# Strided attention: an output partition with 16 queries of two heads, and the turned weights in a block matrix

## The chip, the cores and the metric

The kernel runs on one core of a Trainium2 chip. The metric is the device time of one execution in microseconds; of the kernel before there are three runs. One further execution was recorded by the profiler; the views below are of that one. A core has four compute engines, each with its own queue of instructions: TensorE (PE, matmuls), VectorE (DVE), ScalarE (ACT) and GpSimd (POOL). SyncE (SP) issues the transfers, which 16 DMA engines carry out.

## The reference

Each query attends to every 64th position alone, 16 keys per head:

```python
# Q, K, V: (8, 12, 1024, 64) float32; stride = 64
scale = 1.0 / np.sqrt(64)
for i in range(1024):
    k = K[:, :, 0:1024:stride]          # 16 keys of a head
    v = V[:, :, 0:1024:stride]
    scores = einsum('bhqd,bhkd->bhqk', Q[:, :, i:i+1], k) * scale
    weights = exp(scores - max(scores))
    weights = weights / (sum(weights) + 1e-10)
    result[:, :, i] = einsum('bhqk,bhkd->bhqd', weights, v)
```

Q is read and the result written in full, 24 MiB each. Of K and V only the rows in use are read, 384 KB each.

## The kernel before

The 96 heads are cut into 24 groups of four (`HG = 4`). A group's queries are 4 x 1024 rows of 64 numbers, 1 MiB; they lie in HBM one after the other, so partition p of a query tile `qn` holds 32 successive queries of one head, and each head takes 32 partitions. There are ten query tiles (`QBUFS`) and eight output tiles (`OBUFS`). Each group passes these steps; the names are those of the code:

1. `load`: SP moves the group's queries to `qn`.
2. `cast`: to bf16 in `qb`, a quarter on ACT and three quarters on POOL, in an order that puts the four heads' queries beside each other. `transpose`: VectorE turns blocks of 32 x 32 (pairs of bf16 as int32) into `qt`.
3. `scores`: PE, sixteen matmuls (eight tiles of 128 queries by the even and odd halves of the 64 dimensions) against the group's keys in `k_t`, 64 columns each (four heads x 16 keys), into one PSUM bank `sc`.
4. `lowered`: VectorE takes the maximum of each 16 and subtracts it; `raised`: ACT's exponential; `sums`: VectorE's sums and reciprocals; `weights`: POOL multiplies, giving bf16 weights `wn`, 128 x 512.
5. `across`: PE, four matmuls turn `wn` block by block against a permutation matrix `spread`, so that (head, key) lies along the partitions and queries along the columns. Two tiles of 64 (head, key) rows lie one below the other in each block, in the PSUM bank `wt_ps`.
6. `weight_rows`: ACT copies `wt_ps` to `wt` in bf16 (one instruction, L443).
7. `outputs` (L453): PE, eight matmuls. The stationary operand is one tile's 64 rows x 128 queries of `wt`, the moving operand the same 64 rows of `vm`, a matrix in which each head's 16 value rows stand in that head's columns and zeros elsewhere (64 rows x 256 columns, in two copies one below the other). The result, 128 queries x four heads x 64, goes to half a bank of `o_ps`. The first four matmuls fill two banks (key `o0`), the others the remaining two (`o1`).
8. `evict` (L466): ACT copies two banks at a time to the output tile, two instructions of 1024 columns.
9. `store`: SP writes the tile, alone in the first ten groups, mostly two groups at once after that. An output partition holds 8 queries of each of the four heads, so a store writes runs of 8 x 64 x 4 bytes = 2 KiB in HBM.

The groups overlap. In turn `i` the program writes out, in this order: `weight_rows(i)`, `transpose(i + 3)`, `cast(i + 4)`, `sums(i + 1)`, `scores(i + 2)`, `lowered(i + 2)`, `values(i + 1)`, `weights(i + 1)`, `outputs(i)`, `evict(i)`, `raised(i + 2)`, `across(i + 1)`, then the loads and stores. Every engine works through its own part of that order without overtaking. So ACT's queue in a turn is the weight copy, the cast, the two evictions, the exponential; PE's is scores, output products, turning. The class `Program` derives the semaphore waits from the tiles that each step reads and writes. PE and VectorE run the middle turns as a hardware loop of two turns (`PERIOD = 2`); the other engines' instructions are written out. The products of `outputs(i)` wait on the semaphore `evened`, which `weight_rows(i)` raises; the first eviction waits for the first four products and, from the ninth group on, for the store that last used the output tile.

Ahead of the loop stand the set-up of the constants (`identity`, `perm_v`, `spread`, `mask`, the cleared `k_t`), the keys' way into `k_t` (`key_rows`, `keys`), and `value_rows`, in which four matmuls of 384 columns (L344) copy the value rows to all partitions that need them.

Of the kernel before, what the change touches and what calls it, by code (L numbers as in the profile page):

```python
# [10 lines left out]
FP32 = mybir.dt.float32  # L11
BF16 = mybir.dt.bfloat16
# [190 lines left out]
def kernel(  # L203
# [8 lines left out]
    nc = tc.nc  # L212

    B, H, S, D = Q.shape
    NK = S // stride
    scale = 1.0 / math.sqrt(D)

    P = 128
    HG = 4
    NG = B * H // HG  # L220
    NC = NG // 2
    SD = S * D
    HK = HG * NK
    NT = 8
    PERIOD = 2
    assert B * H == NG * HG and S == 1024 and D == 64 and NK == 16 and NG % PERIOD == 0
    QBUFS = 10
    OBUFS = 8
    AHEAD = 4

    sb = ctx.enter_context(tc.tile_pool(name="sb", bufs=1))
# [6 lines left out]
    identity = sb.tile([P, P], BF16, name="identity")  # L238
    qn = [sb.tile([P, 32 * D], FP32, name=f"qn{i}") for i in range(QBUFS)]
    qb = [sb.tile([P, 32 * D], BF16, name=f"qb{i}") for i in range(2)]  # L240
    out_all = [sb.tile([P, 2, HG, NT, D], FP32, name=f"out_sb{i}") for i in range(OBUFS // 2)]
    out_sb = [out_all[i // 2][:, i % 2] for i in range(OBUFS)]
    qt = [sb.tile([P, 32 * D], BF16, name=f"qt{i}") for i in range(2)]
    low = [sb.tile([P, NT * HG, NK], FP32, name=f"low{i}") for i in range(2)]
    ex = [sb.tile([P, NT * HG, NK], FP32, name=f"ex{i}") for i in range(2)]
    wn = [sb.tile([P, NT * HG, NK], BF16, name=f"wn{i}") for i in range(2)]
    wt = [sb.tile([P, NT // 2, P], BF16, name=f"wt{i}") for i in range(2)]
    top = sb.tile([P, NT * HG], FP32, name="top")
    total = sb.tile([P, NT * HG], FP32, name="total")
    rec = [sb.tile([P, NT * HG], FP32, name=f"rec{i}") for i in range(2)]  # L250
    vm = [sb.tile([P, HG, D], BF16, name=f"vm{i}") for i in range(2)]
    k_t = sb.tile([P, NG, 2, HK], BF16, name="k_t")
    k_r = sb.tile([P, NC, D], BF16, name="k_r")
    v_bf = sb.tile([P, NC, D], BF16, name="v_bf")
    v_rep = sb.tile([P, NC, 2, D], BF16, name="v_rep")
    perm_v = sb.tile([P, 2, 2, HK], BF16, name="perm_v")
    spread = sb.tile([P, P], BF16, name="spread")
    s_sel = sb.tile([P, HG], BF16, name="s_sel")
    mask = sb.tile([P, HG, D], BF16, name="mask")
    sc_ps = [ps.tile([P, 512], FP32, name=f"sc{i}") for i in range(2)]  # L260
    wt_ps = [ps.tile([P, 512], FP32, name=f"wt_ps{i}") for i in range(2)]
    o_ps = ps.tile([P, 4, 512], FP32, name="o")

    prog = Program(nc, tc, PERIOD, (NG - 4) // PERIOD)
    op = prog.op
    stored = {}
    did = {}
# [17 lines left out]
    for g in range(1, QBUFS):  # L285
# [4 lines left out]
        out=identity, in_=identity, compare_op=ALU.not_equal, fill=1.0, base=0,  # L290
        pattern=[[-1, P]], channel_multiplier=1,
    ), reads=["identity"], writes=["identity"])
    for c in range(2):
        op("POOL", lambda c=c: nc.gpsimd.tensor_copy(
            out=perm_v[:, c],
            in_=identity[:, HK * c : HK * c + HK].unsqueeze(1).to_broadcast([P, 2, HK]),
        ), reads=["identity"], writes=[f"perm{c}"])
    op("POOL", lambda: nc.gpsimd.tensor_copy(
        out=spread.rearrange("p (q j) -> p q j", j=4),
        in_=identity.rearrange("p (j q) -> p q j", j=4),  # L300
    ), reads=["identity"], writes=["spread"])
    op("DVE", lambda: nc.vector.memset(k_t, 0.0),  # L302
       writes=[f"k_t{m}{c}{s}" for m in range(2) for c in range(2) for s in range(4)])
    op("DVE", lambda: nc.vector.tensor_reduce(
        out=s_sel, in_=identity.rearrange("p (h s k) -> p s h k", h=2, s=4),
        op=ALU.max, axis=mybir.AxisListType.XY,
# [16 lines left out]
    def keys(m, c, s):  # L323
        part = halves[m]
        hd = 2 * (s % 2) + s // 2
        src, dst, col = 32 * (2 * c + s % 2), 32 * hd, NK * hd
        e, fn = (
            ("DVE", nc.vector.tensor_copy) if m else
            ("POOL", nc.gpsimd.tensor_copy) if s >= 2 else ("ACT", nc.scalar.copy)
        )  # L330
        op(e, lambda: fn(  # L331
            k_t[dst : dst + 32, 2 * part.start + c : 2 * part.stop : 2, :, col : col + NK],
            k_r[src : src + 32, part].rearrange(
                "p n (a k f) -> p a n f k", a=2, f=2
            )[:, s // 2],
        ), reads=[f"k_r{m}"] + ["mask", "turn"] * (e == "POOL"),
           writes=[f"k_t{m}{c}{s}"] + ["turn"] * (e == "POOL"))

    def value_rows(n):
        rows = o_ps[:, 2 * n : 2 * n + 2, 0 : NC // 2 * D].rearrange("p c (n d) -> p c n d", d=D)  # L340

        def sums():
            for c in range(2):
                r = nc.tensor.matmul(  # L344
                    rows[:, c], lhsT=perm_v[:, c].rearrange("p a k -> p (a k)"),
                    rhs=v_bf[:, 6 * n : 6 * n + 6], start=True, stop=True,
                )
            return r

        i = op("PE", sums, reads=["v_bf", "perm0", "perm1"],  # L350
               writes=[f"o{n}"], gates=[did["v_bf"]], gate="scored")
        op("DVE", lambda: nc.vector.tensor_copy(  # L352
            out=v_rep[:, 6 * n : 6 * n + 6].rearrange("p n c d -> p c n d"), in_=rows
        ), reads=[f"o{n}"], writes=[f"v_rep{n}"], gates=[i])
# [5 lines left out]
            op=ALU.mult,  # L360
        ), reads=["mask", "v_rep0", "v_rep1"], writes=[f"vm{g % 2}"])

    cut = 6

    def cast(g):
        q = qn[g % QBUFS].rearrange("p (j t d) -> p t j d", j=4, t=NT)
        b = qb[g % 2].rearrange("p (t j d) -> p t j d", t=NT, j=4)
        one = op("ACT", lambda: nc.scalar.copy(b[:, cut:], q[:, cut:]),  # L368
                 reads=[f"qn{g % QBUFS}1"], writes=[f"qb{g % 2}1"], gate="copied")
        two = op("POOL", lambda: nc.gpsimd.tensor_copy(out=b[:, :cut], in_=q[:, :cut]),  # L370
                 reads=[f"qn{g % QBUFS}0"] + ["turn"] * (g < 2),
                 writes=[f"qb{g % 2}0"] + ["turn"] * (g < 2), gate="cast")
        did["cast", g] = [one, two]
# [8 lines left out]
    def scores(g, i=None):  # L382
        def products(i=None):
            k = g if i is None else i + 2
            q = qt[g % 2]
            for x in range(NT):
                t = x // 4 * 4 + x % 2 * 2 + x // 2 % 2
                for f in range(2):
                    r = nc.tensor.matmul(  # L389
                        sc_ps[g % 2][:, HK * x : HK * x + HK],  # L390
                        lhsT=q[:, 4 * D * t + f : 4 * D * (t + 1) : 2],
                        rhs=k_t[:, k, f], start=f == 0, stop=f == 1,
                    )
# [46 lines left out]
            gates=[did["weighed", g]], turn=i)  # L440

    def weight_rows(g):
        did["evened", g] = op("ACT", lambda: nc.scalar.copy(  # L443
            wt[g % 2], wt_ps[g % 2].rearrange("p (b q) -> p b q", b=NT // 2),
        ), reads=[f"wt_ps{g % 2}"], writes=[f"wt{g % 2}"], gate="evened")

    def outputs(g, i=None):
        for n in range(2):
            def products(i=None, n=n):
                for x in range(4 * n, 4 * n + 4):  # L450
                    b, side = x // 2, x % 2
                    rows = slice(HK * side, HK * side + HK)
                    r = nc.tensor.matmul(  # L453
                        o_ps[:, 2 * n + side, HG * D * (b % 2) : HG * D * (b % 2 + 1)],
                        lhsT=wt[g % 2][rows, b],
                        rhs=vm[g % 2][rows].rearrange("p h d -> p (h d)"),
                        start=True, stop=True,
                    )
                return r

            op("PE", products, reads=[f"wt{g % 2}", f"vm{g % 2}"], writes=[f"o{n}"],
               gates=[] if n else [did["evened", g]], turn=i)

    def evict(g):
        for n in range(2):
            op("ACT", lambda n=n: nc.scalar.copy(  # L466
                out_sb[g % OBUFS][:, :, 4 * n : 4 * n + 4].rearrange("p h t d -> p t h d"),
                o_ps[:, 2 * n : 2 * n + 2].rearrange("p b (t h d) -> p (b t) h d", t=2, h=HG),
            ), reads=[f"o{n}"], writes=[f"out{g % OBUFS}{n}"],
               after=[stored[g - OBUFS]] if g >= OBUFS and not n else [],  # L470
               last=n == 1 and g + 1 == NG)

    def send(g, n):
        o = out_sb[g % OBUFS]
        return _copy(
            nc,
            _ap_with(out, [[NT * D, P], [SD, HG * n], [1, NT * D]], g * HG * SD),
            _ap_with(o, [o.ap[0], [1, 1], [1, 32 * n * D]]),
        )

# [100 lines left out]
```

## Time and profile before

| | us |
|---|---|
| median of three runs | 129.01 (128.92 to 129.18) |
| the profiled execution | 128.92 |
| its span in the profile | 127.1 |

| Engine | busy us | share of the span |
|---|---|---|
| DVE | 88.9 | 70% |
| ACT | 86.6 | 68% |
| POOL | 78.5 | 62% |
| PE | 63.6 | 50% |
| DMA queue of SP | | 96.7% of 16 engines |

The span is the time from the first to the last instruction that the profile holds; the rest of an execution's time lies around it. In rows of instructions, the line of the code comes with the engine and the operation, then the tiles (output <- inputs) and their sizes as partitions x elements. `128*128` or `64*128` beside a matmul is the part of the PE array that it takes, rows first. In a row of the timeline, the first number is the start in us from the span's beginning, the second the duration; `x8` means that eight instructions stand in one row, and a bracket gives idle time ahead of it and what ended it. In a row of the waits stand the total in us, the number of times and the longest one. The ends of matmuls are modelled, their starts are recorded.

### The profile page before, as it was taken

How to read it: one execution, taken by the hardware profiler on the slowest of the kernel's cores; microseconds unless marked ns; L12 is line 12 of the kernel's file. 1: busy time of each engine (PE TensorE's matmuls, PEld its weight loads, DVE VectorE, ACT ScalarE, POOL GpSimd, SP SyncE). 2: the span in 40 equal slices, each digit the busy share in tenths (PEclk: the TensorE clock that was granted, in tenths of full speed). 3: DMA queues.
4: the chain of work that ended last, by engine and by line, in shares of the span. 5: the costliest groups of instructions: out<-in, count | busy, mean ns of one | idle time of the engine just before them, and what ended most of it. 6: DMA issues, size and time to landing. Idle time of an engine off the chain costs nothing.

```text
span 127.1 us, 2044 instructions
## 1 busy us (share of the span) xinstructions
PE 63.6 (50%) x676; PEld 41.9 (33%) x676; DVE 88.9 (70%) x134; ACT 86.6 (68%) x127; POOL 78.5 (62%) x87
## 2 busy tenths in 40 slices
PE   0003607658576766857766564564565477450000
PEld 0002405535254543624544334244244245220000
DVE  4259899998898989989898965965966895500000
ACT  4431316998989899898998568577586977775000
POOL 4264789898787888878789747748649433320000
DMA  2998999999999799999999899898999999999991
GB/s 50 411 433 371 474 433 392 495 392 428 433 392 495 322 405 454 392 438 446 392 456 456 361 487 433 356 490 363 436 407 433 428 412 420 418 418 423 399 415 41
DMA packets 6853, 51.17 MB, mean 402 GB/s; under 512 B 3776, under 2 KB 3776, under 8 KB 3776
## 3 DMA queue, kind: packets, MB, share of 16 engines
q1 hardware_dynamic: 6848, 51.12, 96.7%
q14 instruction: 4, 0.03, 0.1%
q8 instruction: 1, 0.02, 0.0%
HBM read 25.95 MB, written 25.17 MB: 402 GB/s over the span
## 4 chain that ended last, share of the span: by engine, by line
DMA 38%; ACT 21%; PE 10%; DVE 10%; POOL 5%; issue 4%; SPq 2%; ACTq 0%; DVEq 0%; POOLq 0%
DMA out_dram<-out_sb 31%; ACT out_sb L466 16%; DMA qn<-in_Q_dram 7%; PE o L453 4%; PE sc L389 3%; POOL wn L423 3%; ACT ex L411 3%; DVE total L416 3%; DVE qt L378 3%; PE wt_ps L432 2%; ACT wt L443 2%; DVE rec L419 2%; DVE v_rep L352 1%; POOL qb L370 1%; SPq L34 1%
## 5 line engine op out<-in xcount | busy, mean ns | idle before, releaser
L466 ACT COPY out_sb<-o 128x1024 f32<-128x1024 f32 x48 | 46.2, 1015 | 16.1 <-DMA out_dram<-out_sb 8.8
L423 POOL TENSOR_TENSOR wn<-ex,rec 128x512 bf16<-128x512 f32 x24 | 25.4, 1057 | 25.9 <-DVE rec L419 25.9
L370 POOL CAST qb<-qn 128x1536 bf16<-128x1536 f32 x24 | 35.2, 1468 | 3.8 <-DMA qn<-in_Q_dram 3.7
L389 PE MATMUL sc<-k_t,qt 128*128 (+1 forms) x384 | 25.8, 242 | 14.9 <-DVE qt L378 10.4
L453 PE MATMUL o<-vm,wt 64*128 64x256 bf16 x192 | 24.8, 411 | 14.8 <-ACT wt L443 14.7
L378 DVE STREAM_TRANSPOSE qt<-qb 128x1024 int32<-128x1024 int32 x24 | 29.8, 1240 | 2.9 <-POOL qb L370 1.5
L389 PEld LDWEIGHTS sc<-k_t,qt 128*128 128x128 bf16 x384 | 23.2, 131 | 18.1 <-DVE qt L378 10.4
L416 DVE TENSOR_REDUCE total<-ex 128x32 f32<-128x512 f32 x24 | 16.2, 674 | 12.8 <-ACT ex L411 12.8
L432 PE MATMUL wt_ps<-spread,wn 128*128 128x128 bf16 x96 | 14.6, 307 | 19.0 <-POOL wn L423 19.0
L368 ACT CAST qb<-qn 128x512 bf16<-128x512 f32 x24 | 15.2, 635 | 5.4 <-DMA qn<-in_Q_dram 5.4
L411 ACT ACTIVATE ex<-low 128x512 f32<-128x512 f32 x24 | 15.4, 642 | 4.3 <-DVE low L405 4.3
L432 PEld LDWEIGHTS wt_ps<-spread,wn 128*128 128x128 bf16 x96 | 8.3, 131 | 30.1 <-POOL wn L423 30.1
L453 PEld LDWEIGHTS o<-vm,wt 64*128 64x128 bf16 x192 | 10.5, 127 | 21.2 <-ACT wt L443 17.7
L405 DVE TENSOR_TENSOR low<-sc,top 128x512 f32<-128x512 f32 x24 | 16.6, 692 | 0.8
L357 POOL TENSOR_TENSOR vm<-mask,v_rep 128x256 bf16<-128x256 bf16 x24 | 16.1, 670 | 0.0
L402 DVE TENSOR_REDUCE top<-sc 128x32 f32<-128x512 f32 x24 | 15.2, 633 | 0.0
L443 ACT CAST wt<-wt_ps 128x512 bf16<-128x512 f32 x24 | 14.1, 587 | 0.0
L419 DVE RECIPROCAL rec<-total 128x32 f32<-128x32 f32 x24 | 8.5, 353 | 0.8
L302 DVE MEMSET k_t<- 128x1536 uint32 x1 | 1.3, 1338 | 1.9 <-issue 1.9
L344 PE MATMUL o<-v_bf,perm_v 128*128 128x384 bf16 x4 | 1.5, 521 | 2.3 <-POOL v_bf L501 2.3
L316 ACT CAST k_bf<-k_raw 128x256 bf16<-128x256 f32 (+1 forms) x2 | 0.9, 508 | 2.3 <-DMA k_raw<-in_K_dram 2.3
L331 POOL COPY k_t<-k_r 32x128 bf16<-32x128 bf16 x4 | 1.1, 288 | 2.1 <-DVE k_r L318 2.0
(17 smaller groups left out, 11.0 us busy)
## 6 DMA issues: line engine op xcount, KB each, us to landing
qn<-in_Q_dram SPq DMA_DIRECT2D x24, 1024.0 KB, 19.1
out_dram<-out_sb SPq DMA_DIRECT2D x12, 1024.0 KB, 19.6
out_dram<-out_sb SPq DMA_DIRECT2D x6, 2048.0 KB, 19.6
k_raw<-in_K_dram SPq DMA_DIRECT2D x1, 384.0 KB, 4.0
v_raw<-in_V_dram SPq DMA_DIRECT2D x1, 384.0 KB, 6.5
```

The lines of the kernel that those rows point to most:

```text
L357: op("POOL", lambda: nc.gpsimd.tensor_tensor(out=vm[g % 2], in0=mask, in1=v_rep[:, g // 2, g % 2].unsqueeze(1).to_broadcast([P, HG, D]), o ...
L370: two = op("POOL", lambda: nc.gpsimd.tensor_copy(out=b[:, :cut], in_=q[:, :cut]), reads=[f"qn{g % QBUFS}0"] + ["turn"] * (g < 2), writes=[ ...
L378: "DVE", lambda: nc.vector.transpose(qt[g % 2].bitcast(I32), qb[g % 2].bitcast(I32)),
L389: r = nc.tensor.matmul(sc_ps[g % 2][:, HK * x : HK * x + HK], lhsT=q[:, 4 * D * t + f : 4 * D * (t + 1) : 2], rhs=k_t[:, k, f], start=f == ...
L405: op("DVE", lambda: nc.vector.tensor_tensor(out=low[g % 2], in0=sc, in1=top.unsqueeze(2).to_broadcast([P, NT * HG, NK]), op=ALU.subtract,) ...
L411: did["raised", g] = op("ACT", lambda: nc.scalar.activation(out=ex[g % 2], in_=low[g % 2], func=AF.Exp, bias=0.0, scale=scale,), reads=[f" ...
L416: added = op("DVE", lambda: nc.vector.tensor_reduce(out=total, in_=ex[g % 2], op=ALU.add, axis=mybir.AxisListType.X,), reads=[f"ex{g % 2}" ...
L423: did["weighed", g] = op("POOL", lambda: nc.gpsimd.tensor_tensor(out=wn[g % 2], in0=ex[g % 2], in1=rec[g % 2].unsqueeze(2).to_broadcast([P ...
L432: r = nc.tensor.matmul(wt_ps[g % 2][:, P * b : P * b + P], lhsT=w[:, P * b : P * b + P], rhs=spread, start=True, stop=True,)
L443: did["evened", g] = op("ACT", lambda: nc.scalar.copy(wt[g % 2], wt_ps[g % 2].rearrange("p (b q) -> p b q", b=NT // 2),), reads=[f"wt_ps{g ...
L453: r = nc.tensor.matmul(o_ps[:, 2 * n + side, HG * D * (b % 2) : HG * D * (b % 2 + 1)], lhsT=wt[g % 2][rows, b], rhs=vm[g % 2][rows].rearra ...
L466: op("ACT", lambda n=n: nc.scalar.copy(out_sb[g % OBUFS][:, :, 4 * n : 4 * n + 4].rearrange("p h t d -> p t h d"), o_ps[:, 2 * n : 2 * n + ...
```

## The change

The pairing of queries and heads changes from the cast on. A tile of 128 queries is now taken so that an output partition ends up with 16 queries of two heads (`NU = 16`) where it had 8 of four; a store then writes runs of 16 x 64 x 4 bytes = 4 KiB. The four heads of a group are handled as two pairs, and for that:

- the casts' orders, `spread`, the columns of the keys in `k_t`, the value permutation `perm_v` (four small copies, not two) and the PSUM columns of the scores follow the new order; each pair of score products still fills 64 columns, now in two runs of 32;
- `wt` becomes a block matrix: for each of four blocks and both halves `u` of its queries, 128 rows x 128 columns, in which the rows 0 to 63 have data in the columns 0 to 63 and the rows 64 to 127 in the columns 64 to 127. The rest is zero, from one VectorE memset ahead of the loop (`wt_all`);
- `weight_rows` fills the two diagonal blocks with one ACT copy each, of 64 partitions x 512; the second one raises `evened`;
- `outputs` still has eight matmuls of 256 columns, but each uses all 128 rows;
- `evict` and `store` follow the new layout; the number and the size of the evictions, loads and stores stay.

```diff
+    NU = 16
...
-    out_all = [sb.tile([P, 2, HG, NT, D], FP32, name=f"out_sb{i}") for i in range(OBUFS // 2)]
+    out_all = [sb.tile([P, 2, 2, NU, D], FP32, name=f"out_sb{i}") for i in range(OBUFS // 2)]
...
-    wt = [sb.tile([P, NT // 2, P], BF16, name=f"wt{i}") for i in range(2)]
+    wt_all = sb.tile([P, 2, NT // 2, 2, P], BF16, name="wt_all")
+    wt = [wt_all[:, i] for i in range(2)]
...
+    id_v = identity.rearrange("p (c b a k) -> p c b a k", c=2, b=2, a=2)
     for c in range(2):
-        op("POOL", lambda c=c: nc.gpsimd.tensor_copy(
-            out=perm_v[:, c],
-            in_=identity[:, HK * c : HK * c + HK].unsqueeze(1).to_broadcast([P, 2, HK]),
-        ), reads=["identity"], writes=[f"perm{c}"])
+        for a in range(2):
+            op("POOL", lambda c=c, a=a: nc.gpsimd.tensor_copy(
+                out=perm_v[:, c, a],
+                in_=id_v[:, c, :, a].unsqueeze(1).to_broadcast([P, 2, 2, NK]),
+            ), reads=["identity"], writes=[f"perm{c}{a}"])
     op("POOL", lambda: nc.gpsimd.tensor_copy(
-        out=spread.rearrange("p (q j) -> p q j", j=4),
-        in_=identity.rearrange("p (j q) -> p q j", j=4),
+        out=spread.rearrange("p (u q h) -> p u q h", u=2, h=2),
+        in_=identity.rearrange("p (u h q) -> p u q h", u=2, h=2),
     ), reads=["identity"], writes=["spread"])
...
+    op("DVE", lambda: nc.vector.memset(wt_all, 0.0), writes=[f"wt{i}" for i in range(2)])
...
-        src, dst, col = 32 * (2 * c + s % 2), 32 * hd, NK * hd
+        src, dst, col = 32 * (2 * c + s % 2), 32 * hd, 32 * (s // 2) + NK * (s % 2)
...
-    cut = 6
+    cut = 12
...
-        q = qn[g % QBUFS].rearrange("p (j t d) -> p t j d", j=4, t=NT)
-        b = qb[g % 2].rearrange("p (t j d) -> p t j d", t=NT, j=4)
+        q = qn[g % QBUFS].rearrange("p (h u d) -> p u h d", h=2, u=NU)
+        b = qb[g % 2].rearrange("p (u h d) -> p u h d", u=NU, h=2)
...
+            sc = sc_ps[g % 2].rearrange("p (b a t k) -> p b t a k", b=NT // 2, a=2, t=2)
             for x in range(NT):
-                t = x // 4 * 4 + x % 2 * 2 + x // 2 % 2
                 for f in range(2):
                     r = nc.tensor.matmul(
-                        sc_ps[g % 2][:, HK * x : HK * x + HK],
-                        lhsT=q[:, 4 * D * t + f : 4 * D * (t + 1) : 2],
+                        sc[:, x // 2, x % 2], lhsT=q[:, 4 * D * x + f : 4 * D * (x + 1) : 2],
                         rhs=k_t[:, k, f], start=f == 0, stop=f == 1,
                     )
...
     def weight_rows(g):
-        did["evened", g] = op("ACT", lambda: nc.scalar.copy(
-            wt[g % 2], wt_ps[g % 2].rearrange("p (b q) -> p b q", b=NT // 2),
-        ), reads=[f"wt_ps{g % 2}"], writes=[f"wt{g % 2}"], gate="evened")
+        for a in range(2):
+            rows = slice(HK * a, HK * a + HK)
+            did["evened", g] = op("ACT", lambda rows=rows: nc.scalar.copy(
+                wt[g % 2][rows, :, :, rows],
+                wt_ps[g % 2][rows].rearrange("p (b u q) -> p b u q", b=NT // 2, u=2),
+            ), reads=[f"wt_ps{g % 2}"], writes=[f"wt{g % 2}{a}"], gate="evened" if a else None)
...
-                for x in range(4 * n, 4 * n + 4):
-                    b, side = x // 2, x % 2
-                    rows = slice(HK * side, HK * side + HK)
-                    r = nc.tensor.matmul(
-                        o_ps[:, 2 * n + side, HG * D * (b % 2) : HG * D * (b % 2 + 1)],
-                        lhsT=wt[g % 2][rows, b],
-                        rhs=vm[g % 2][rows].rearrange("p h d -> p (h d)"),
-                        start=True, stop=True,
-                    )
+                for b in range(2 * n, 2 * n + 2):
+                    o = o_ps[:, b].rearrange("p (t u c) -> p u t c", t=2, u=2)
+                    for u in range(2):
+                        r = nc.tensor.matmul(
+                            o[:, u], lhsT=wt[g % 2][:, b, u],
+                            rhs=vm[g % 2].rearrange("p (t c) d -> p t (c d)", t=2),
+                            start=True, stop=True,
+                        )
...
-                out_sb[g % OBUFS][:, :, 4 * n : 4 * n + 4].rearrange("p h t d -> p t h d"),
-                o_ps[:, 2 * n : 2 * n + 2].rearrange("p b (t h d) -> p (b t) h d", t=2, h=HG),
+                out_sb[g % OBUFS][:, :, NT * n : NT * n + NT].rearrange("p c u d -> p u c d"),
+                o_ps[:, 2 * n : 2 * n + 2].rearrange("p b (u c d) -> p (b u) c d", u=4, c=2),
...
-            _ap_with(out, [[NT * D, P], [SD, HG * n], [1, NT * D]], g * HG * SD),
+            _ap_with(out, [[NU * D, P], [2 * SD, 2 * n], [1, NU * D]], g * HG * SD),
```

More of the change, by code (lines that the diff above doesn't have):

```diff
@@ L255 @@
     v_rep = sb.tile([P, NC, 2, D], BF16, name="v_rep")
-    perm_v = sb.tile([P, 2, 2, HK], BF16, name="perm_v")
+    perm_v = sb.tile([P, 2, 2, 2, 2, NK], BF16, name="perm_v")
     spread = sb.tile([P, P], BF16, name="spread")
@@ L344, in sums @@
                 r = nc.tensor.matmul(
-                    rows[:, c], lhsT=perm_v[:, c].rearrange("p a k -> p (a k)"),
+                    rows[:, c], lhsT=perm_v[:, c].rearrange("p a e b k -> p (a e b k)"),
                     rhs=v_bf[:, 6 * n : 6 * n + 6], start=True, stop=True,
@@ L348, in sums @@
             return r
-        i = op("PE", sums, reads=["v_bf", "perm0", "perm1"],
+        i = op("PE", sums, reads=["v_bf"] + [f"perm{c}{a}" for c in range(2) for a in range(2)],
                writes=[f"o{n}"], gates=[did["v_bf"]], gate="scored")
@@ L449, in products @@
             def products(i=None, n=n):
-                for x in range(4 * n, 4 * n + 4):
-                    b, side = x // 2, x % 2
-                    rows = slice(HK * side, HK * side + HK)
-                    r = nc.tensor.matmul(
-                        o_ps[:, 2 * n + side, HG * D * (b % 2) : HG * D * (b % 2 + 1)],
-                        lhsT=wt[g % 2][rows, b],
-                        rhs=vm[g % 2][rows].rearrange("p h d -> p (h d)"),
-                        start=True, stop=True,
-                    )
+                for b in range(2 * n, 2 * n + 2):
[6 more added lines that the diff above has]
+                        )
                 return r
-            op("PE", products, reads=[f"wt{g % 2}", f"vm{g % 2}"], writes=[f"o{n}"],
+            op("PE", products, reads=[f"wt{g % 2}", f"wt{g % 2}0", f"wt{g % 2}1", f"vm{g % 2}"], writes=[f"o{n}"],
                gates=[] if n else [did["evened", g]], turn=i)
```

## The prediction

> **What bounds the kernel now.** I read the page first, for the busy shares and the DMA queue; then the stretches of the span; the list of waits; and last the chain that ended last, lap by lap.
>
> ```profile
> span 127.1 us, 2044 instructions
> ...
> PE 63.6 (50%) x676; PEld 41.9 (33%) x676; DVE 88.9 (70%) x134; ACT 86.6 (68%) x127; POOL 78.5 (62%) x87
> ...
> q1 hardware_dynamic: 6848, 51.12, 96.7%
> ```
> ```profile
> 72.00:97.00 25.00, 13.76 (x150) 9.12 (x149) 18.03 (x26) 17.49 (x26) 15.98 (x16) 1.00 1.01 424
> ```
> The last two columns of the stretch are the DMA engines' share and their GB/s (a share is counted by the packets that begin in a stretch, so it can pass 1). The transfers fill the span: 0.967 x 127.1 = 122.9 us of work for the 16 engines, which leaves idle time at the two ends alone. The computing has slack; how much, the waits and a lap tell.
>
> ```profile
> ACT out_sb L466 <- DMA out_dram<-out_sb: 8.8, 6, 1.6
> ```
> ```profile
> 20.31 0.58 ACT L443 CAST wt<-wt_ps 128x512 bf16<-128x512 f32 x1
> ```
> ```profile
> 103.82 1.93 ACT out_sb L466 x2
> 105.75 0.53 ACT ex L411
> 106.27 0.48 ACT wt L443
> 106.76 0.05 issue
> 106.80 0.63 PE o L453 x4
> 107.43 0.02 issue
> 107.45 1.79 ACT out_sb L466 x2
> ...
> 114.20 1.93 ACT out_sb L466 x2
> ```
> Rows give start and duration. ScalarE (ACT) waited six times, 8.8 us in all, for an output buffer that a store still held: in those groups the transfers pace it. Elsewhere it runs in a closed lap of its own: two evictions, exponential, copy of the turned weights, the first four output products on TensorE (PE), and evictions again. From 103.82 to 107.45 that is 3.63 us. The row at 20.31 is the weight copy of the first of the 24 groups, the one at 114.20 holds the last evictions. They end at 116.1, and 11 us of stores are still to go.
>
> Against the lap stand the transfers of a group, one load and one store, 2 x 1.05 MB, at 424 GB/s 4.95 us. The lap is shorter, so ScalarE runs ahead until the buffers are full. This slack is what a longer lap spends.
>
> **The stores.** They stay 1 MiB a group; only their runs in HBM double, from 2 to 4 KiB. Two windows of the DMA view, 12 to 31 us with load packets alone and 90 to 122 with store packets alone, give the price of a run (packets, MB, share):
>
> ```profile
> q1 hardware_dynamic: 373, 8.03, 98.3%
> ```
> ```profile
> q1 hardware_dynamic: 998, 13.38, 100.2%
> ```
> Per busy time the loads make 8.03 / (0.983 x 19) = 430 GB/s, the stores 13.38 / (1.002 x 32) = 417. A load moves 8 KiB runs on its SBUF side (32 queries x 64 numbers x 4 bytes), a store 2 KiB runs on its HBM side. All stores, 24 x 1.05 = 25.2 MB, cost 60.3 us; at the loads' rate it would be 58.5. If a run has a fixed cost, doubling its length takes off half of that, and the loads still pay a quarter of it: (1/2) / (3/4) = two thirds of 1.8, so 1.2 us. Ends: nothing (the difference is not one of runs) and 1.8. I take 1.2. That lowers the floor that the transfers set from 127.1 to 125.9 us of span. The Trainium skill ("DMA: Bandwidth & Descriptors", Specifications) puts the least transfer for full rate at 512 B. By that rule 2 KiB runs lose nothing and the floor stays at 127.1. The rates of 430 and 417 speak for a small loss instead.
>
> **The copy in two halves.** One copy of 128 partitions x 512 becomes two of 64 x 512. What counts is whether fewer partitions make it cheaper:
>
> ```profile
> L331 ACT COPY k_t<-k_r 32x128 bf16<-32x128 bf16 x4 | 1.2, 294 | 0.1
> ```
> ```profile
> L316 ACT CAST k_bf<-k_raw 128x512 bf16<-128x512 f32 x1 | 0.6, 612 | 0.0
> ```
> ```profile
> L316 ACT CAST k_bf<-k_raw 128x256 bf16<-128x256 f32 x1 | 0.4, 404 | 2.3 <-DMA k_raw<-in_K_dram 2.3
> ```
> On 128 partitions 256 more columns cost 208 ns; carried down to 128 columns that is 404 - 104 = 300 ns, and 32 partitions took 294. So a half copy costs what a whole one does. Instructions overlap at their ends, as a lap in the middle shows:
>
> ```profile
> 57.47 0.64 ACT L411 ACTIVATE ex<-low 128x512 f32<-128x512 f32 x1
> 58.00 0.59 ACT L443 CAST wt<-wt_ps 128x512 bf16<-128x512 f32 x1
> 58.47 0.64 ACT L368 CAST qb<-qn 128x512 bf16<-128x512 f32 x1
> 59.55 1.93 ACT L466 COPY out_sb<-o 128x1024 f32<-128x1024 f32 x2 [0.45 <-PE o L453]
> ```
> The cast starts 58.47 - 58.00 = 0.47 after the copy. The second half adds 0.47 us to the lap (0.46 to 0.59, the latter without overlap). Nothing covers it: the output products wait for the second half, and the evictions wait for them. Behind it in ScalarE's queue stand the cast of a later group, the evictions and the next exponential.
>
> **The output products.** Eight matmuls on 64 rows become eight on all 128, each still 256 columns wide. The same lap on PE, four full-row products of 384 columns, and the means of one product:
>
> ```profile
> 56.78 0.61 PE L432 MATMUL wt_ps<-spread,wn 128*128 128x128 bf16 x4 [0.73 <-POOL wn L423]
> 57.86 1.11 PE L389 MATMUL sc<-k_t,qt 128*128 x16 [0.47 <-issue]
> 58.90 1.04 PE L453 MATMUL o<-vm,wt 64*128 64x256 bf16 x8
> ```
> ```profile
> 13.68 1.46 PE L344 MATMUL o<-v_bf,perm_v 128*128 128x384 bf16 x4 [2.29 <-POOL v_bf L501]
> ```
> ```profile
> L453 PE MATMUL o<-vm,wt 64*128 64x256 bf16 x192 | 24.8, 411 | 14.8 <-ACT wt L443 14.7
> ...
> L432 PE MATMUL wt_ps<-spread,wn 128*128 128x128 bf16 x96 | 14.6, 307 | 19.0 <-POOL wn L423 19.0
> ...
> L344 PE MATMUL o<-v_bf,perm_v 128*128 128x384 bf16 x4 | 1.5, 521 | 2.3 <-POOL v_bf L501 2.3
> ```
> Start to start, 128 columns take (0.61 - 0.307) / 3 = 0.10 us and 384 take (1.46 - 0.521) / 3 = 0.31, so 256 on full rows about 0.21. The output products need (1.04 - 0.411) / 7 = 0.09 each. Two 64-row products therefore run side by side, two per 0.21. With 128 rows each stands alone: the four ahead of the first eviction are three steps, 3 x 0.21, where it was one step between two pairs, 0.21. The eviction comes 0.42 us later (bounds: 0, if the products keep their pace; 0.55, if a weight load shows too). All eight now last 7 x 0.21 + 0.41 = 1.88 us; the second eviction, 0.9 after the first, finds its half just ready. The cast between copy and eviction (0.64) ends inside the longer wait and stays hidden.
>
> **The small edits** cost nothing on the path. Score columns go to PSUM in two runs of 32 instead of one of 64, in the same 16 matmuls; the casts (1536 and 512 columns), exponentials, evictions and VectorE's work keep shapes and runs of 64 numbers. One memset more (2048 bf16) and two more small copies stand ahead of the loop, while DVE and POOL wait for the keys:
>
> ```profile
> 1.86 1.34 DVE L302 MEMSET k_t<- 128x1536 uint32 x1 [1.86 <-issue]
> ```
> ```profile
> 5.39 0.31 DVE L318 STREAM_TRANSPOSE k_r<-k_bf 128x128 int32<-128x128 int32 x1 [2.04 <-ACT k_bf L316]
> ```
> The memset has two thirds of the words of k_t's, so 0.9 us, against 2.04 of waiting; without that cover it would cost 0.9 once.
>
> **The sum.** The lap becomes 3.63 + 0.47 + 0.42 = 4.52 us, in both turns of the loop: what lengthens the lap shown in the middle (there the output products waited for the score products, which end at 58.97, and not for the copy, which ends at 58.59) disappears when a second copy ends at 59.06. VectorE and POOL, 88.9 / 24 = 3.7 and 78.5 / 24 = 3.3 us a group, stay under it. From the copy's end to the eviction it is 107.45 - 106.76 = 0.69 now and 1.11 then, so the first eviction starts at 20.31 + 0.47 + 0.58 + 1.11 = 22.5, the twenty-fourth at 22.5 + 23 x 4.52 = 126.5, and that ends at 128.4, against 114.20 + 1.93 = 116.1 now. A lap of 4.52 is below 4.95, so no transfer is in its way while loads last, but after the loads only one store per lap is due, 2.5 us, and the backlog of 11 us melts. The transfers, which could be through at 125.9, then wait for the last groups. From the last eviction to the end:
>
> ```profile
> L34 SPq DMA_DIRECT2D out_dram<-out_sb x18: 538/1569/7307, 24.5 to 116.7; - x18
> ```
> ```profile
> DMA to landing us min/median/max: 9.7/19.6/25.6
> ```
> ```profile
> k_raw<-in_K_dram SPq DMA_DIRECT2D x1, 384.0 KB, 4.0
> ```
> The last store is issued 0.6 us after the last eviction (116.7 against 116.1) and lands 9.7 later, 126.4, with 0.7 left to the end of the span. Alone it needs its data time, 1.05 MB / 425 = 2.5 us, and what surrounds it; the keys, alone too, took 4.0 for 384 KB in small runs. I take 4.0 (2.5 to 5.5). End of span: 128.4 + 0.6 + 4.0 + 0.7 = 133.7. The profiled execution took 128.92 for a span of 127.1, 1.8 outside it, and the median of the runs is 129.01, the same within 0.1%. So 133.7 + 1.8 = 135.5 us, 5% slower: the transfers gain 1.2 that nobody sees, and 24 longer laps take their place as the bound.
>
> **Rivals.** (1) *Faster: the lap stays inside the slack.* The point that decides: for a span of 127.1 the last eviction may end at 121.8, a lap of (121.8 - 1.9 - 22.5) / 23 = 4.23. The copy alone (4.10) is under it. So if full-row products step at 0.11 us, half of 0.21, or hide otherwise, the transfers still bound, and it takes 125.9 + 1.8 = 127.7 us. For it: products would follow each other more densely, outputs, turning and scores for 1.7 + 0.4 + 0.85 of each 4.5 us, and a faster clock would halve every step. Against it: 0.10 for 128 columns at 57 us is the same pace as 0.31 for 384 at 14, so nothing sped up in over 40 us of work in which PE's pauses were like the 0.73 and 0.47 of the lap shown. The Trainium skill ("TensorE: Matmul & The Clock Gate", Part 1) says that some 3.4 us of sustained matmuls lift the gate to 2.4 GHz, and its closing table that gaps under 3 us keep it there. By that rule steps would be 0.11 and the time 127.7; the trace before does not bear it out, since 0.10 us for 128 columns is 1.2 GHz in spite of short pauses. I give this rival 0.15.
> (2) *No change, within 0.2%:* the length of the runs costs nothing (floor 127.1) and the lap stays under 4.23: 129.0. 0.03.
> (3) *Slower, but partly covered:* the first eviction waits only 0.2 us more, lap 4.3: 22.5 + 98.9 + 1.9 + 5.3 + 1.8 = 130.4. 0.07.
> (4) *Slower still:* half copies don't overlap and a weight load shows, lap 4.77: 141. 0.05.
>
> **How the numbers follow.** My case, a lap of 4.45 to 4.65, has 0.70 and gives 133.9 to 138.5. With (3), whose 130.4 I round down to 130, the range is 130 to 138.5 and holds just under 0.8. Faster by over 0.2% (about what a measurement here can tell from no change): 0.15; within 0.2%: 0.03; slower: 0.70 + 0.07 + 0.05 = 0.82.
>
> **What would show it.** After the change the weight copy's line should have 48 copies of about 587 ns, the output products 192 of 128x256 with 1.9 us for eight, ScalarE a wait of some 0.6 us for them in each lap, no wait for out_dram at all, laps near 4.5 us, and DMA digits that fall below 9 in the last quarter. Store packets alone should run at about 425 GB/s. I am wrong if the wait for out_dram stays, if steps of 0.11 appear in the products, or if the last eviction ends before 122 us.

## The result: 3.7% slower, and the bound moves from the transfers to ScalarE's lap

| | before | after |
|---|---|---|
| median | 128.96 us (4 runs, 128.90 to 129.18) | 133.92 us (4 runs, 133.43 to 134.03) |
| profiled execution, its span | 128.92, 127.1 | 133.99, 132.2 |

The ratio is 1.037 with a 95% interval of [1.034, 1.039]. First the page of the changed kernel, the lines that answer to those of before:

```profile
span 132.2 us, 2072 instructions
...
PE 70.3 (53%) x676; PEld 52.6 (40%) x676; DVE 90.5 (69%) x135; ACT 102.1 (77%) x151; POOL 78.8 (60%) x89
...
PEclk9999999985559955599559555586557975785555
DMA  2999999999998999989989989989999987709945
...
q1 hardware_dynamic: 6848, 51.12, 92.3%
```

The DMA digits fall from nines to 7, 0 and 4 in the last fifth of the span: the transfers have caught up with ScalarE and wait for it. Their own work is 0.923 x 132.2 = 122.0 us where it was 122.9. ScalarE is busy 15.5 us longer. And there is a line that the page of before did not have: PEclk, the clock that TensorE was granted, switches between full (9) and half (5) from the tenth slice on. Its first nines are no measurement, since the views print full speed until the first event of the clock: the first group's four output products, at 21.81, took 1.05 us, as they do at half speed later.

The waits of ScalarE, and its lap in the chain that ended last (start and duration in us):

```profile
ACT out_sb L472 <- PE o L460: 9.4, 15, 1.1
```
```profile
29.02 0.53 ACT ex L415
29.55 0.46 ACT wt_all L449
30.01 0.01 issue
30.02 0.59 ACT wt_all L449
30.61 0.05 issue
30.65 1.05 PE o L460 x4
31.70 0.02 issue
31.73 1.93 ACT out_sb L472 x2
...
38.29 0.53 ACT ex L415
38.82 0.46 ACT wt_all L449
39.27 0.01 issue
39.28 0.59 ACT wt_all L449
39.87 0.05 issue
39.92 0.62 PE o L460 x4
40.55 0.02 issue
40.57 1.01 ACT out_sb L472
...
124.67 1.93 ACT out_sb L472 x2
```

No wait of ScalarE for `out_dram` is left, though it was 8.8 us before. The chain is the lap from the first group (eviction at 22.89) to the last (124.67). Two lengths of lap occur: from the evictions' end at 29.02 to the next evictions at 31.73 it is 2.71 us, from 38.29 to 40.57 it is 2.28. With 1.93 for the evictions that makes 4.63 (4.64 by the rounded rows) and 4.21. They differ in one row alone, the first four output products: 1.05 or 0.62. The row at 30.65 lies in a slice of PEclk 5, the one at 39.92 in a slice of 9. Twelve laps have the one length, ten the other, and the last, without an exponential, is 4.12: 12 x 4.63 + 10 x 4.21 + 4.12 = 101.8 = 124.67 - 22.89.

### The profile page after: what moved, and what is told of

Same layout as the page of the kernel before. It is cut to its first block, busy times and chain, and to the rows that moved or that the text cites. A ratio compares the mean times of both kernels' runs of the same rounds, so it can differ in the third digit from the quotient of the medians.

```text
span 132.2 us, 2072 instructions
## 1 busy us (share of the span) xinstructions
PE 70.3 (53%) x676; PEld 52.6 (40%) x676; DVE 90.5 (69%) x135; ACT 102.1 (77%) x151; POOL 78.8 (60%) x89
## 4 chain that ended last, share of the span: by engine, by line
ACT 57%; PE 16%; issue 8%; DMA 6%; DVE 4%; POOL 2%; SPq 1%; POOLq 0%
ACT out_sb L472 28%; ACT wt_all L449 19%; PE o L460 16%; ACT ex L415 10%; DMA qn<-in_Q_dram 6%; DVE v_rep L357 1%; POOL qb L375 1%; DVE qt L383 1%; SPq L281 1%; PE o L349 1%; POOL v_bf L507 1%; SPq L34 1%; DVE low L409 1%; DVE total L420 0%; DVE top L406 0%
## 5 line engine op out<-in xcount | busy, mean ns | idle before, releaser
L460 PE MATMUL o<-vm,wt_all 128*128 128x256 bf16 x192 | 36.9, 358 | 33.8 <-ACT wt_all L449 33.8
L460 PEld LDWEIGHTS o<-vm,wt_all 128*128 128x128 bf16 x192 | 21.6, 123 | 43.3 <-ACT wt_all L449 37.5
L394 PE MATMUL sc<-k_t,qt 128*128 (+1 forms) x384 | 24.3, 234 | 13.9 <-DVE qt L383 10.6
L394 PEld LDWEIGHTS sc<-k_t,qt 128*128 128x128 bf16 x384 | 21.6, 126 | 16.5 <-DVE qt L383 10.6
L449 ACT CAST wt_all<-wt_ps 64x512 bf16<-64x512 f32 x48 | 27.6, 575 | 0.3
L436 PE MATMUL wt_ps<-spread,wn 128*128 128x128 bf16 x96 | 13.2, 282 | 5.1 <-POOL wn L427 3.7
L436 PEld LDWEIGHTS wt_ps<-spread,wn 128*128 128x128 bf16 x96 | 9.5, 131 | 9.7 <-POOL wn L427 8.1
L336 DVE COPY k_t<-k_r 32x256 bf16<-32x256 bf16 x8 | 2.3, 285 | 0.2
```

The lines of the kernel that those rows point to most:

```text
L394: r = nc.tensor.matmul(sc[:, x // 2, x % 2], lhsT=q[:, 4 * D * x + f : 4 * D * (x + 1) : 2], rhs=k_t[:, k, f], start=f == 0, stop=f == 1,)
L436: r = nc.tensor.matmul(wt_ps[g % 2][:, P * b : P * b + P], lhsT=w[:, P * b : P * b + P], rhs=spread, start=True, stop=True,)
L449: did["evened", g] = op("ACT", lambda rows=rows: nc.scalar.copy(wt[g % 2][rows, :, :, rows], wt_ps[g % 2][rows].rearrange("p (b u q) -> p ...
L460: r = nc.tensor.matmul(o[:, u], lhsT=wt[g % 2][:, b, u], rhs=vm[g % 2].rearrange("p (t c) d -> p t (c d)", t=2), start=True, stop=True,)
```

## Experiments

Experiments 1 to 6 and 10 change one thing of the kernel before or of the changed one; 7 to 9 change two, and say which. In the diffs, `...` stands for code that is left out.

**1 and 2. The runs alone.** The kernel before, with nothing but the store's address pattern changed:

```diff
-            _ap_with(out, [[NT * D, P], [SD, HG * n], [1, NT * D]], g * HG * SD),
+            _ap_with(out, [[2 * NT * D, P], [2 * SD, 2 * n], [1, 2 * NT * D]], g * HG * SD),    # 4 KiB
+            _ap_with(out, [[HG * NT * D, P], [HG * SD, n], [1, HG * NT * D]], g * HG * SD),     # 8 KiB
```

Expected, 4 KiB: 

> The kernel before with the store's address pattern alone changed to runs of 4 KiB; the same bytes leave, the rows land in another order than the reference's. Theory (a run has a fixed cost, the transfers set the end): in the changed kernel a 1 MiB store's packets were about 2% shorter and the DMA queue's total fell from 122.9 to 122.0 us, so the time falls by 0.9 to 1.2 us, to 127.8 to 128.1, the lap of ScalarE staying at 3.6 to 3.9. Rival (2 KiB runs already go at full rate): 129.0, within 0.2%.

Expected, 8 KiB: 

> The kernel before with the store's pattern changed to runs of 8 KiB, one per partition and group; the rows land in another order than the reference's. Theory (a fixed cost per run): half of what 4 KiB gained is added, 1.4 to 1.8 us under the kernel before, 127.3 to 127.6. Rival (the runs cost nothing beyond 4 KiB): the same as with 4 KiB, 128.0. Rival (no cost of runs at all): 129.0.

Measured: 128.09 us for 4 KiB against 129.04, ratio 0.993 [0.990, 0.995]; 128.08 for 8 KiB, 0.993 [0.990, 0.996]. Repeated later, 4 KiB gave 128.13, 0.993 [0.991, 0.996]. In a window with store packets alone, 98 to 113 us, the queue's packets, MB and share are, for 2, 4 and 8 KiB (kernel before, then the two):

```profile
q1 hardware_dynamic: 430, 6.26, 100.0%
```
```profile
q1 hardware_dynamic: 436, 6.36, 100.0%
```
```profile
q1 hardware_dynamic: 444, 6.47, 101.2%
```

Per busy time of the 15 us that is 417, 424 and 426 GB/s. The first doubling gave 0.95 us, as the theory said. The second gave a little more rate and no time that these runs can tell apart, so the fixed cost per run, as the only term, fell with it: the third value should have been near 428, and another 0.5 us faster. The rival without any cost of runs is out.

**3. The split copy alone.** The kernel before with two copies of 64 partitions:

```diff
-        did["evened", g] = op("ACT", lambda: nc.scalar.copy(
-            wt[g % 2], wt_ps[g % 2].rearrange("p (b q) -> p b q", b=NT // 2),
-        ), ...
+        for a in range(2):
+            rows = slice(HK * a, HK * a + HK)
+            did["evened", g] = op("ACT", lambda rows=rows: nc.scalar.copy(
+                wt[g % 2][rows], wt_ps[g % 2][rows].rearrange("p (b q) -> p b q", b=NT // 2),
+            ), ..., gate="evened" if a else None)
...
```

Expected: 

> The kernel before with the weight copy in two halves of 64 partitions and nothing else changed: the output products stay on 64 rows, the stores at 2 KiB. Theory: the lap becomes 3.64 + 0.58 = 4.2 us (the second copy measured 0.58 in the changed kernel, with no overlap), the last evictions end at 22.3 + 23 x 4.2 + 1.9 = 121, and 5.6 us later, at 126.6, all would be done, just inside the transfers' 127.1: 129.0, within 0.5%. Rival (the copy alone makes the changed kernel slow, the products add nothing): about 133.5, as the changed kernel.

Measured: 128.92 us, ratio 0.999 [0.997, 1.001]. Its laps are 4.21 (the last, which has no exponential, 3.69). ScalarE's timeline shows one:

```profile
57.83 0.64 ACT L411 ACTIVATE ex<-low 128x512 f32<-128x512 f32 x1
58.36 1.16 ACT L445 CAST wt<-wt_ps 64x512 bf16<-64x512 f32 x2
59.55 0.62 ACT L368 CAST qb<-qn 128x512 bf16<-128x512 f32 x1
60.23 1.93 ACT L468 COPY out_sb<-o 128x1024 f32<-128x1024 f32 x2
```

A lap 0.58 us longer in every group costs nothing by itself: the slack holds it, just, for of ScalarE's waits for `out_dram`, 8.8 us before, none is left. The rival that the copy alone makes the change slow is out.

**4. The full-row products alone.** The changed kernel with one copy of all partitions into the first 64 columns of the block matrix:

```diff
-        for a in range(2):
-            ...
+        did["evened", g] = op("ACT", lambda: nc.scalar.copy(
+            wt[g % 2][:, :, :, 0:HK],
+            wt_ps[g % 2].rearrange("p (b u q) -> p b u q", b=NT // 2, u=2),
+        ), ..., gate="evened")
```

Expected: 

> The changed kernel with one weight copy of 128 partitions x 512 that puts all rows into the first 64 columns of the block matrix, where the changed kernel has two copies; the output mixes wrong rows, every other step is kept. Theory: the lap loses the 0.58 us of the second copy: 3.64 while TensorE's steps are 0.11, 4.06 while they are 0.21, both under 4.23; the transfers set the end with 4 KiB runs: 127.8 to 128.1. Rival (the full-row products alone are enough to make it slow): above 130.

Measured: 128.19 us against 128.95, ratio 0.994 [0.992, 0.996]. ScalarE waits for buffers again:

```profile
ACT out_sb L470 <- PE o L458: 14.8, 22, 1.5
...
ACT out_sb L470 <- DMA out_dram<-out_sb: 2.3, 2, 1.5
```

So the products alone fit in the slack as well, and the gain of the longer runs shows. Neither the copy nor the products make the kernel slow; the two together do, because they spend the same slack.

**5 and 6. The clock.** The changed kernel with more work for TensorE. The turning matmuls are repeated into the same place, three and five times; they stand behind the output products in TensorE's queue, off ScalarE's lap:

```diff
-            for b in range(NT // 2):
+            for b in 3 * list(range(NT // 2)):     # and 5 *
                 r = nc.tensor.matmul(
                     wt_ps[g % 2][:, P * b : P * b + P], lhsT=w[:, P * b : P * b + P],
```

Expected, three times: 

> The changed kernel with every turning matmul of the weights (four a group) done three times over, into the same place, so TensorE has 0.43 to 0.86 us more work a lap, off ScalarE's lap. In the changed kernel's trace the laps come in two lengths, 4.21 us where the granted clock is 1.0 and 4.63 where it is 0.5. Theory (the clock gate follows how busy TensorE is): the clock stays up in more laps, more of them take 4.21; with all of them 22.9 + 23 x 4.21 + 1.9 + 5.6 + 1.8 = 129.0, so between 129.0 and 132.5, faster than the changed kernel's 133.9 though work is added. Rival (clock and extra work unrelated): 133.9 or more.

Expected, five times: 

> The changed kernel with the four turning matmuls done five times over (16 extra matmuls a group, 1.7 us of TensorE at the low clock, 0.9 at the high one). With three times, 19 of 23 laps took about 4.21 and the time fell to 131.98. Theory (the clock gate follows how busy TensorE is): nearly all laps take 4.21, at or under three times' 131.98, down to 129.0. Rival (the extra work now stands in the lap's way, the score products come late): laps over 4.63 and 134 or more.

Measured: 131.98 us with three (four executions, 131.07 to 133.19), ratio to the kernel before 1.026 [1.020, 1.032], and 130.03 with five, 1.009 [1.006, 1.013], against 1.037 [1.034, 1.039] with one. The page's clock line of the two, and of the latter the group of the output products:

```profile
PEclk9999999998599999999657999999995599955865
```
```profile
PEclk9999999999999999999999999999999999999965
```
```profile
L460 PE MATMUL o<-vm,wt_all 128*128 128x256 bf16 x192 | 25.2, 274 | 28.3 <-ACT wt_all L449 28.3
```

With five the clock stays up over the whole loop, every full lap is 4.21 us (4.20 in some), and the products' mean is 274 ns where it was 358. Work added to a queue that is off the path made the kernel 3.9 us faster. That it is not the 129.0 of the expectation lies at the start: the first group's weights wait for their twenty turning matmuls, and the first eviction begins at 24.34, not 22.89. In the full laps with five ScalarE no longer waits for the output products (it does so four times, 2.8 us in all, where it was 15 times and 9.4), so 4.21 is ScalarE's own work. The theory that the clock follows how busy TensorE is stands; how much work it takes was not measured more finely than these three steps.

**7. The layout without the block matrix.** The changed kernel with one copy of all partitions, and each product of 128 rows cut into two that use a quarter of the array each (the diff shows the products):

```diff
...
-                        r = nc.tensor.matmul(
-                            o[:, u], lhsT=wt[g % 2][:, b, u],
-                            rhs=vm[g % 2].rearrange("p (t c) d -> p t (c d)", t=2),
+                        for a in range(2):
+                            rows = slice(HK * a, HK * a + HK)
+                            r = nc.tensor.matmul(
+                                o[rows, u], lhsT=wt[g % 2][rows, b, u],
+                                rhs=vm[g % 2][rows].rearrange("p (t c) d -> p t (c d)", t=2),
...
```

Expected: 

> The changed kernel's layout and its 4 KiB runs, but without the block matrix: one weight copy of 128 partitions, and each output product of 128 rows cut into two of 64 rows x 64 columns, the upper rows writing output partitions 0 to 63, the lower 64 to 127. Theory: two such products run side by side, so four steps stand ahead of the first eviction (0.42 us more than before) and no second copy: lap 3.64 + 0.42 = 4.06 or, with the clock up, 3.64. Both are inside the slack of 4.23, the transfers set the end with the longer runs: 127.8 to 128.1. Rival (the four-way cut of the array runs the products one after the other): 16 x 0.21 us, lap near 5, 143 or more.

Measured: 128.82 us against 129.04, ratio 0.998 [0.997, 1.000]. A lap of its chain:

```profile
104.17 1.93 ACT out_sb L470 x2
106.09 0.53 ACT ex L413
106.62 0.48 ACT wt L445
107.11 0.04 issue
107.15 1.08 PE o L458 x8
108.23 0.02 issue
108.25 1.41 ACT out_sb L470 x2
```

Eight products stand ahead of the eviction and take 1.08 us, as four did with the block matrix: they run in pairs. The lap, 108.25 - 104.17 = 4.08, is what was expected, and ScalarE again waits for buffers, twice, 2.0 us in all. The whole slowdown is undone with this layout. But 127.8 to 128.1 was expected and 128.82 came; so something else had grown.

**8 and 9. What the 0.7 us are.** The kernel before with runs of 4 KiB, once with the turning three times over, once with eight matmuls of two columns a group added, each written over by the real one right after (the diff shows this second edit, without the stores):

```diff
             for b in range(NT // 2):
-                r = nc.tensor.matmul(
-                    wt_ps[g % 2][:, P * b : P * b + P], lhsT=w[:, P * b : P * b + P],
-                    rhs=spread, start=True, stop=True,
-                )
+                for n in (2, 2, P):
+                    r = nc.tensor.matmul(
+                        wt_ps[g % 2][:, P * b : P * b + n], lhsT=w[:, P * b : P * b + P],
+                        rhs=spread[:, 0:n], start=True, stop=True,
+                    )
```

Expected, three times: 

> The kernel before with runs of 4 KiB and the turning matmuls done three times; the rows land in another order than the reference's. It asks why the version with products of 64 x 64 took 128.82 where the runs of 4 KiB alone took 128.09, though the transfers set the end of both. Theory (the number and the density of TensorE's instructions cost nothing while the lap is inside the slack): 128.1. Rival (more matmuls make the transfers' end later by themselves): 128.6 to 129.

Expected, two columns: 

> The same with eight matmuls of two columns each added to the turning of every group, written over by the real ones right after: as many instructions more as with the turning done three times (which took 128.69), but nearly no streaming. Theory A (the mere number of TensorE's instructions makes the end later): 128.6 to 128.8. Theory B (it is how long TensorE streams): 128.1, as the control.

The repeat of 4 KiB served as the control: 

> The kernel before with runs of 4 KiB once more, as the control of the next one (the rows land in another order than the reference's): 128.1, 0.7% under the kernel before.

Measured: 128.69 us with the threefold turning (0.998 [0.996, 0.999]) and 128.62 with two columns (0.997 [0.995, 0.999]), against 128.09 and 128.13 without. My theory (hidden work costs nothing) fell in the one, and theory B in the other: 192 more matmuls with their 192 weight loads (2428 instructions in the page, 2044 without) cost about 0.5 us although the transfers set the end and the matmuls hardly stream. The 64 x 64 products add as many (2430) and lose 0.7. In the profile of the two-column version the span ends 0.4 us later than its control's (126.7 against 126.3) with the last transfers. In which way instructions of TensorE delay them, these runs don't show. So no version here that computes the right result has both the layout and the gain of its longer runs.

**10. Where the copies' overlap went.** The kernel before with two copies of all 128 partitions and 256 columns each:

```diff
-        did["evened", g] = op("ACT", lambda: nc.scalar.copy(
-            wt[g % 2], wt_ps[g % 2].rearrange("p (b q) -> p b q", b=NT // 2),
+        for a in range(2):
+            part = slice(2 * a, 2 * a + 2)
+            did["evened", g] = op("ACT", lambda part=part: nc.scalar.copy(
+                wt[g % 2][:, part], wt_ps[g % 2].rearrange("p (b q) -> p b q", b=NT // 2)[:, part],
...
```

Expected: 

> The kernel before with the weight copy in two instructions of all 128 partitions x 256 columns. In the version with two halves of 64 partitions the second copy began 0.58 us after the first, which lasted 0.57: no overlap, where other neighbours on ScalarE overlap by 0.10 to 0.12. Theory A (it is the change of partitions that ends the overlap): the second copy begins about 0.26 after the first, which lasts 0.37, and the lap is 3.9. Theory B (a second instruction without a wait of its own has no overlap): it begins 0.38 after it, and the lap is 4.0.

Measured in a single execution (128.7 us):

```profile
58.09 0.65 ACT L445 CAST wt<-wt_ps 128x256 bf16<-128x256 f32 x2
58.61 0.65 ACT L368 CAST qb<-qn 128x512 bf16<-128x512 f32 x1
59.53 1.93 ACT L468 COPY out_sb<-o 128x1024 f32<-128x1024 f32 x2 [0.27 <-PE o L455]
```

Both copies together take 0.65 us, little more than the 0.59 of the whole, and the cast begins 0.13 before they end. Two halves of 64 partitions take 1.16, and in experiment 3 the cast begins 0.03 after their end. So two instructions in a row without a wait between them do overlap, and theory B is out. Theory A, that a change of partitions ends the overlap, is too wide: in the rows of experiment 3 the first half copy begins 0.11 before the end of the exponential (58.36 against 57.83 + 0.64), although the partitions change there too, from 128 to the lower 64. The overlap is lost on both sides of the copy of the upper half. Whether its start at partition 64 is the reason was not tested. My lap of 3.9 for it was wrong all the same: I had added a half copy, where the other half had become shorter too; it is 3.70 in one turn of the loop and 3.8 in the other.

## Why the prediction was right, and which terms were off

- **The bound changes.** Right: the lap left the slack, the wait for `out_dram` went from 8.8 us to none, the DMA digits fell at the end, and the end is that of ScalarE's chain.
- **The second copy, 0.47 us.** Mis-sized: 0.58. The number of partitions hardly matters for one copy's length (575 ns for 64 against 587 for 128), as read from the keys' rows. But I took the overlap from neighbours on all 128 partitions, and the copy of the upper half has none (experiments 3 and 10).
- **The output products, 0.42 us.** Right at the low clock: 1.05 against 0.63 us, and the step of 0.21 shows in eight of them lasting 1.89. At the full clock the first four take 0.62 and add nothing.
- **The lap, 4.52.** It came out as 4.63 and 4.21, 4.43 in the mean of 23, since one term was too small and the other was paid in 13 of them only. The sum also gave the last lap an exponential that it doesn't have, 0.5 us. In all the laps took 2.2 us less than forecast, the start 0.4 and the tail 0.3 more; 135.5 was forecast, 133.9 measured. That it came so near owes something to errors of opposite sign: the mean lap lies just under 4.45, where my case began.
- **The start and the tail.** The first eviction began at 22.89, not 22.5 (0.11 of it by the copy; the first copy itself began at 20.58, not 20.31, as the second load landed 0.25 later). The last store, alone at the end, landed 4.2 us after its issue (4.0 forecast); from the last eviction's end at 126.6 to the span's end it took 5.6 us (5.3 forecast).
- **The stores, 1.2 us that nobody sees.** 0.9 by the queue's own time, 0.95 when seen alone (experiment 1). The rule of 512 B for full rate (the Trainium skill, "DMA: Bandwidth & Descriptors", Specifications) does not hold for these stores: 417 GB/s at 2 KiB, 424 at 4, 426 at 8.
- **Rival 1, the clock.** I had given it 0.15 as all or nothing. It came, for ten laps of 23, and the run is closer to the kernel before because of it. With it came one of my signs of being wrong, steps of 0.11 us in the products: they show where four take 0.62, so my mechanism is the whole story in the laps at half speed alone. Its price was wrong: 127.7 came from a lap of 4.10, but with the copy at 0.58 a full clock means 4.21, just at the threshold of 4.23, and experiment 6 took 130.0 with its extra work. What spoke against it, that nothing sped up in the kernel before, was true of its profiled execution and did not bear on a TensorE with more to do.
- **Rivals 2 and 3** did not happen: the runs do cost something, and the first eviction's wait was 0.42 or none and not 0.2. **Rival 4** came by half: the halves don't overlap, but no weight load showed.

## What to carry to other kernels

Slack is one account for all edits: the copy (0.58 a lap) and the wider products (0.42) were each free and together cost 4%, so the sum of an edit's hidden costs is to be held against the lap that the bound allows, here 4.23 us. Zeros that are there only to fill a matrix cost the copy that must go round them and the array rows that they take; placing the products in parts of the array gave the same layout without either, though twice as many matmuls went with 0.7 us at the end. And a lap that waits for TensorE is to be costed at both clocks, with the question which of them the change will bring.

## What the runs showed of the hardware

**A clock that follows the load, at short pauses.** In the profiled execution of the kernel before, 128 columns step at 0.10 us throughout, half speed. More streaming lifted the clock: with the changed kernel for parts of the time, with three times the turning for most of it, with five times all through the loop:

```profile
23.00:72.00 49.00, 31.16 (x315) 23.59 (x314) 38.56 (x56) 45.81 (x67) 34.51 (x35) 0.72 1.00 423
```
```profile
23.00:72.00 49.00, 33.37 (x415) 26.53 (x413) 39.41 (x57) 46.83 (x69) 35.19 (x35) 0.90 0.99 420
```
```profile
23.00:72.00 49.00, 33.87 (x511) 27.77 (x509) 40.16 (x58) 47.79 (x70) 35.34 (x35) 1.00 0.99 421
```

These are the same stretch of the three, with the busy us of TensorE, its weight loads, VectorE, ScalarE and GpSimd and the number of their instructions; the third number from the right is the mean granted clock, 0.72, 0.90 and 1.00, for 315, 415 and 511 matmuls (the one to three us ahead of the first event of the clock count as 1.00). What it takes is not the number of matmuls. The two versions of experiments 8 and 9 add 192 each. At the same stage of the loop sixteen score products take 1.11 us (half speed) in the version with two columns and 0.63 in the one with 128:

```profile
58.24 1.11 PE L389 MATMUL sc<-k_t,qt 128*128 x16 [0.26 <-issue]
```
```profile
59.96 0.63 PE L389 MATMUL sc<-k_t,qt 128*128 x16
```

Nor is it short pauses. TensorE's waits for the copied weights (total, times, longest) in the kernel before, in the changed one and with five times the turning:

```profile
PE o L453 <- ACT wt L443: 14.7, 16, 1.8
```
```profile
PE o L460 <- ACT wt_all L449: 33.8, 24, 2.6
```
```profile
PE o L460 <- ACT wt_all L449: 28.3, 24, 1.7
```

The rule that pauses under 3 us keep the clock up (the Trainium skill, "TensorE: Matmul & The Clock Gate", closing table) is not borne out: the changed kernel's clock falls again and again in the loop at waits of 2.6 us at most, and with five times the turning it stays up at waits as long as those of the kernel before. How much TensorE streams goes with the clock; whether the share of the time decides, or the length of a burst, these runs don't separate. Nor is it the same each time: with runs of 8 KiB (experiment 2), where TensorE has the work of the kernel before, the clock came up twice for about 3 us, and four turning matmuls took 0.40 us at 34.38 where they take 0.61 at 38.00:

```profile
PEclk9999999999955555555555955555555555555555
```

Where the profile has no event of the clock, as in the kernel before, or none yet, its views print 1.00, though the steps are those of half speed; the steps are to be read, not the column.

**Neighbouring instructions of ScalarE overlap by 0.10 to 0.12 us, but not on either side of a copy of the upper 64 partitions**: 0.58 from start to start for copies of 0.57, and 0.03 between its end and the cast.

**Matmuls that nobody waits for are not free**: 192 more of two columns, 0.5 us at the end, with the lap inside its slack.
